# A fp32 diffusion step on one core: when the weight sums of seven-product blocks are made, where the last such block stands, and how the closing norm's factors are built

## The chip, the core and the metric

The kernel runs on one core of a Trainium2 chip. The metric is the device time of one execution in microseconds, the median of several runs. Five engines work side by side, each on its own queue in order: TensorE (PE, with its weight loads PEld), VectorE (DVE), ScalarE (ACT), GpSimd (POOL) and SyncE (SP), which here issues most DMAs.

## The reference

One layer of a hybrid diffusion backbone runs over 128 context tokens and 256 latent tokens with 2048 channels. A mixing sub-layer comes first (gated linear attention, a Fourier branch, gates). What matters here is the second sub-layer and its norm:

```python
h = rmsnorm(x, lw['norm_pre_ffn']) * (1.0 + sc2) + sh2
ff = (jax.nn.silu(h @ lw['w_ffn_gate']) * (h @ lw['w_ffn_up'])) @ lw['w_ffn_down']
x = x + ga2 * rmsnorm(ff, lw['norm_post_ffn'])
```

The hidden width is 5632. Everything is fp32.

## The kernel before, in words

**Split products.** Every fp32 operand is split into two parts, hi and lo, and a product is three matmuls: hi with hi, hi with lo, lo with hi. A weight tile of 128x1024 arrives by DMA (`raw`, two buffers, or `u`/`u3s`, below), ACT casts it to `whi` (L1324), DVE subtracts to get `wlo` (L1325), and PE uses both. `whi` and `wlo` have four buffers each: when PE takes weight k, the split of weight k+3 is queued (`grab2`, L1330).

**The stages of the feed-forward layer.** The 5632 hidden channels are 11 chunks of 4 tiles. In each chunk there are gate projections g0 to g3 and up projections u0 to u3 of 48 matmuls each (L275, moving 128x384), and the hidden tile is made by ACT (SiLU) and DVE (`hfE`, L1349), then split (`hid_hi` on ACT, `hid_lo` on DVE). The down projection of a chunk is done one chunk later, in two blocks: the order is written out in `ffn_order` (L172 on). The first block (`d`, half 0) stands behind u1 of the next chunk, the second (`d`, half 1) behind g3.

**A seven-product block.** For the 256 latent tokens a block multiplies two-by-two pieces by a scheme of seven products instead of eight; the context tokens are done plainly beside it. A block has eight weights: four loaded ones, here called U0 to U3 (`uraw`, three in the tile `u`, one in `u3s`), and four made from them in place, T0 to T3. `combine(n)` (L1310) makes one of four sums on DVE, n = 0 and 1 on L1313, 2 and 3 on L1314: they overwrite, in turn, the places of U2, U1, U0 and U3. A sum may run only when the weight in its place has been split. T0, T1, T2, T3 are the places of U2, U1, U0, U3 after their sums. The block is 66 matmuls of 128x512 (L1379), in PSUM tiles `pdn`, added to `psums` (and parts of `u3s`) in SBUF by DVE (L1401, `out`), or copied there by ACT in chunk 1. Before the change `split_next` makes sum n just ahead of the split that precedes Tn's.

**Other work on DVE.** In most chunks DVE also accumulates a modulation column (`adacc`, L573) at fixed places. Seven additions that close the scheme after its last block wait in a list, `pend` (L1426); each weight that is taken pops one.

**The end.** The last chunk's down projection is done in four plain stages (`e`, 36 matmuls each, tiles `pde`, three token tiles t = 0, 1, 2). Each tile is added to its place by DVE (`tail_step`, L1437), ACT squares it and sums along the row into `ssq` (L1438), and DVE adds that to `r3` (L1440). After the last stage each token's factor is made from `r3` (square root on ACT, L1483, reciprocal on DVE, L1486), put on a diagonal matrix `dg` (L1488), and PE multiplies `psums` by it (`py`, L1511): this scales and transposes at once. A "turn" is one such product of one 128x128 piece; in the trace it is two passes of PE, as it is plain fp32. Output k of 16 needs three turns, t = 0, 1, 2; eight `py` buffers exist. DVE (L1537) or, for five of the 16, ACT and POOL (L1529, L1530) apply the last gate and the residual `x1b`, which SP reloads (L1453) into the place of the normalised input, and SP or ACT stores the result.

**What sets the order.** PE, ACT, DVE and POOL run in the order in which the code is written. SP's order is set by a scheduler until the last stage.

Of the kernel before, what the change touches and what calls it, by code (L numbers as in the profile page):

```python
# [14 lines left out]
AF = mybir.ActivationFunctionType  # L15
# [6 lines left out]
D = 2048  # L22
# [12 lines left out]
FC = 4  # L35
# [61 lines left out]
def tile_step(ctx: ExitStack, tc: tile.TileContext, a, o):  # L97
# [941 lines left out]
    with ExitStack() as s:  # L1039
# [245 lines left out]
        pend = []  # L1285

        def load_more():
            n = 0
# [27 lines left out]
        def split_next():  # L1316
            if not entries:
                return
            e = entries.pop(0)
            if entries and entries[0][0] == "T":  # L1320
                combine(entries[0][1])
            raw = e[1] if e[0] == "R" else uraw[(2, 1, 0, 3)[e[1]]]
            hi, lo = (wp.tile([P, G], F32R, tag=t, name=t, bufs=4) for t in ("whi", "wlo"))
            ACT.copy(hi, raw)  # L1324
            DVE.tensor_sub(lo, raw, hi.bitcast(F32))  # L1325
# [12 lines left out]
        hid, sgs, hfs = {}, {}, {}  # L1338
# [93 lines left out]
        r3 = pf.tile([P, 3], F32, name="r3")  # L1432
        dg = pf.tile([P, 3, P], F32, name="dg")

        def tail_step(t, n, p, done):

            DVE.tensor_add(f_at(t, n), f_at(t, n), p)  # L1437
            ACT.activation(hfs[NFC][:, 0:512], f_at(t, n), AF.Square, accum_out=ssq[:, t, done : done + 1])  # L1438
            if done:
                DVE.tensor_add(r3[:, t : t + 1], ssq[:, t, 0:1] if done == 1 else r3[:, t : t + 1], ssq[:, t, done : done + 1])  # L1440

        rate[0] = 0.25
        ada = paced(ada_rest((5,)), rate)
# [1 line left out]
        for kind, c, j in ffn_order[HEAD:]:  # L1445
            if kind == "d":
                down(c, j)
            elif kind == "e":
                if not done:
                    hfs[NFC] = pe.tile([P, FC * T], F32, tag="hf", name="hfE", bufs=1)  # L1450
                    x1b = actp.tile([P, KT, T], F32, tag="A_hi", name="x1b")
                    for q in range(4):
                        SP.dma_start(x1b[:, 4 * q : 4 * q + 4, :], x1_d[:, 4 * q : 4 * q + 4, :])  # L1453
                pool, tag = ((pss, "side"), (psm, "mm"))[done % 2]
                pt = [pool.tile([P, 512], F32, tag=tag, name="pde") for _ in range(3)]
                for kh in range(2):
                    w = grab2()
                    for t in range(3):
                        wmm(pt[t], [h[:, 2 * kh : 2 * kh + 2, t * P : (t + 1) * P] for h in hid[c]], w, kh == 0, kh == 1)
                        if kh:  # L1460
                            if done == 2:
                                while pend:
                                    pend.pop(0)()
                            if done < 3:
                                tail_step(t, j, pt[t], done)
                done += 1
            else:
                if (kind, c, j) == ("u", NFC - 1, FC - 1):
                    for _ in ada:
                        pass  # L1470
                    ACT.activation(tmp1, eps_t, AF.Sqrt)
                proj2(c, j, dst_of[kind])
# [5 lines left out]
        def add_last(t):  # L1478
            DVE.tensor_add(f_at(t, n), f_at(t, n), pt[t])
            ACT.activation(hfs[NFC][:, 0:512], f_at(t, n), AF.Square, accum_out=ssq[:, t, 3:4])  # L1480

        def factors(lo, hi):
            ACT.activation(r3[:, lo:hi], r3[:, lo:hi], AF.Sqrt, bias=eps_t[:, 0:1], scale=1.0 / D)  # L1483

        def diagonals(lo, hi):
            DVE.reciprocal(r3[:, lo:hi], r3[:, lo:hi])  # L1486
            for t in range(lo, hi):
                DVE.tensor_scalar_mul(dg[:, t, :], ident, r3[:, t : t + 1])  # L1488

        def add_ss(t):  # L1490
            DVE.tensor_add(r3[:, t : t + 1], r3[:, t : t + 1], ssq[:, t, 3:4])

        add_last(0)
        add_last(1)
        add_ss(0)
        factors(0, 1)
        add_last(2)
        diagonals(0, 1)
        add_ss(1)
        add_ss(2)  # L1500
        factors(1, 3)
        diagonals(1, 3)

        py = {}
        places = [(pss, "side")] * 5 + [(psm, "mm")] * 3
# [116 lines left out]
```

## Time and profile before

| what | value |
|---|---|
| median of 3 runs | 2020.71 us (2020.23 to 2021.46) |
| the profiled execution | 2022.62 us |
| its span on the core | 2020.8 us |
| PE busy | 1994.4 us, 99% |
| DVE busy | 1476.3 us, 73% |
| ACT busy | 851.6 us, 42% |
| DMA | 380.18 MB, mean 188 GB/s |
| mean granted TensorE clock | 0.997 |

Times inside the trace run from the span's start. A row of the timeline gives start, duration, engine, line, operation and tiles, and in brackets the idle time of the engine before it and what ended it. A duration includes the fill and drain of the engine's pipeline, so two instructions that follow each other without a wait can overlap a little. Matmuls overlap much more: what counts for them is the time from start to start. A row of stretches gives start and end, length, the busy time of each engine (with its number of instructions), the granted clock, the DMA share and GB/s.

### The profile page before, as it was taken

The page shows a single profiled execution, that of the slowest core. Times are in us where ns is not written, and L with a number is a line of the kernel's source. Part 1 is how long each engine was busy: PE and PEld are TensorE (multiplying, and loading weights), DVE is VectorE, ACT ScalarE, POOL GpSimd, SP SyncE. Part 2 cuts the span into 40 slices and gives each one's busy share as a digit, 9 for nine tenths or more (in the row PEclk, how much of TensorE's full clock was granted, in tenths as well). Part 3 has the DMA queues.
Part 4 walks back from the last instruction along what each step waited for, and adds up shares of the span by engine and source line. Part 5 has one row for each costly group of instructions (what it writes and reads, how often), then busy time and mean ns, then how long its engine had stood idle before and what let it go on. Part 6 is the DMA issues. An engine that isn't in the chain of part 4 may idle for free.

```text
span 2020.8 us, 29311 instructions
## 1 busy us (share of the span) xinstructions
PE 1994.4 (99%) x11652; PEld 1870.1 (93%) x11652; DVE 1476.3 (73%) x1892; ACT 851.6 (42%) x1217; POOL 31.3 (2%) x43
## 2 busy tenths in 40 slices
PE   8999999999999999999999999999999999999998
PEld 5779999999999999999999898989899999989986
DVE  5668888888667778866576868676777777766675
ACT  4233554444346544446353433333343333333343
POOL 0000000000000000003000000000000000000000
PEclk9999999999999999999999999999999999999999
DMA  9978777677646686546344445443535454434333
GB/s 390 360 248 268 232 247 249 222 227 249 215 153 222 230 286 194 192 146 225 129 150 143 156 136 167 133 147 130 173 128 165 139 167 138 141 116 135 125 108 143
DMA packets 124521, 380.18 MB, mean 188 GB/s; under 512 B 13788, under 2 KB 32412, under 8 KB 120032
## 3 DMA queue, kind: packets, MB, share of 16 engines
q1 hardware_dynamic: 123664, 377.33, 55.6%
q8 instruction: 91, 1.49, 0.3%
q10 hardware_dynamic: 720, 0.98, 0.1%
q14 instruction: 46, 0.38, 0.1%
HBM read 361.48 MB, written 16.78 MB: 187 GB/s over the span
## 4 chain that ended last, share of the span: by engine, by line
PE 85%; DVE 9%; DMA 3%; ACT 2%; issue 1%; POOL 0%; ACTq 0%; DVEq 0%; POOLq 0%
PE pmm L275 64%; PE pdn L1379 8%; PE pv L416 3%; DVE wlo L1325 3%; DMA raw<-in_w_br_gla 2%; PE pgm L399 2%; DVE psums L1401 1%; DVE u L1313 1%; PE pf L275 1%; PE px L434 1%; PE pmm L1244 1%; DMA raw<-in_w_d 1%; PE py L1511 1%; DVE u3s L1314 1%; DVE u L1314 1%
## 5 line engine op out<-in xcount | busy, mean ns | idle before, releaser
L275 PE MATMUL pmm<-A_hi,whi 128*128 128x384 f32 x2480 | 832.1, 336 | 0.0
L275 PE MATMUL pmm<-A_hi,wlo 128*128 128x384 f32 x2480 | 830.9, 335 | 0.0
L275 PE MATMUL pmm<-A_lo,whi 128*128 128x384 f32 x2480 | 829.0, 334 | 0.0
L275 PEld LDWEIGHTS pmm<-A_hi,wlo 128*128 128x128 f32 x2480 | 465.4, 188 | 4.8 <-DVE wlo L1325 4.8
L275 PEld LDWEIGHTS pmm<-A_hi,whi 128*128 128x128 f32 x2480 | 465.6, 188 | 3.8 <-issue 1.4
L275 PEld LDWEIGHTS pmm<-A_lo,whi 128*128 128x128 f32 x2480 | 465.6, 188 | 1.0
L1325 DVE TENSOR_TENSOR wlo<-raw,whi 128x1024 fp32r<-128x1024 f32 x175 | 214.3, 1225 | 210.4 <-ACT whi L1324 210.2
L1324 ACT CAST whi<-raw 128x1024 fp32r<-128x1024 f32 x175 | 181.7, 1050 | 293.2 <-DMA raw<-in_w_g 138.4
L573 DVE SCALAR_TENSOR_TENSOR adacc<-adaw,spad,adacc 128x1024 f32<-128x1024 f32 x240 | 297.2, 1280 | 0.5 <-DMA adaw<-in_w_ada 0.2
L241 ACT CAST whi<-raw 128x1024 fp32r<-128x1024 f32 x181 | 189.8, 1051 | 196.1 <-DMA raw<-in_w_gate 77.1
L242 DVE TENSOR_TENSOR wlo<-raw,whi 128x1024 fp32r<-128x1024 f32 x179 | 218.1, 1222 | 68.9 <-ACT whi L241 68.6
L1325 DVE TENSOR_TENSOR wlo<-u,whi 128x1024 fp32r<-128x1024 f32 x120 | 146.5, 1222 | 40.0 <-ACT whi L1324 38.6
L1324 ACT CAST whi<-u 128x1024 fp32r<-128x1024 f32 x120 | 126.1, 1051 | 110.2 <-DVE u L1313 32.4
L1379 PE MATMUL pdn<-wlo,hid_hi 128*128 128x512 f32 x280 | 111.2, 397 | 6.5 <-DVE wlo L1325 6.5
L1379 PE MATMUL pdn<-whi,hid_lo 128*128 128x512 f32 x280 | 109.5, 391 | 0.0
L1379 PE MATMUL pdn<-whi,hid_hi 128*128 128x512 f32 x280 | 109.1, 390 | 0.0
L1401 DVE TENSOR_TENSOR psums<-psums,pdn 128x512 f32<-128x512 f32 x126 | 84.0, 685 | 0.0
L1379 PEld LDWEIGHTS pdn<-wlo,hid_hi 128*128 128x128 f32 x280 | 52.5, 188 | 22.8 <-DVE wlo L1325 12.8
L301 ACT CAST hid_hi<-hfE 128x384 fp32r<-128x384 f32 x44 | 22.6, 513 | 112.8 <-DVE hfE L1349 112.8
L1379 PE MATMUL pdn<-wlo,S_hi 128*128 128x512 f32 x160 | 63.3, 396 | 1.4 <-DVE wlo L1325 1.4
L1379 PEld LDWEIGHTS pdn<-whi,hid_hi 128*128 128x128 f32 x280 | 52.6, 188 | 11.0 <-ACT sg L1342 0.4
L1379 PE MATMUL pdn<-whi,S_lo 128*128 128x512 f32 x160 | 62.3, 390 | 0.0
(330 smaller groups left out, 2189.4 us busy)
## 6 DMA issues: line engine op xcount, KB each, us to landing
adaw<-in_w_ada SPq DMA_DIRECT2D x128, 512.0 KB, 4.0
raw<-in_w_g SPq DMA_DIRECT2D x88, 512.0 KB, 4.4
raw<-in_w_u SPq DMA_DIRECT2D x88, 512.0 KB, 4.2
slab<-in_w_ada SPq DMA_DIRECT2D x32, 1024.0 KB
raw<-in_w_gate SPq DMA_DIRECT2D x64, 512.0 KB, 4.5
u<-in_w_d SPq DMA_DIRECT2D x60, 512.0 KB, 4.5
raw<-in_w_in SPq DMA_DIRECT2D x44, 512.0 KB, 3.8
raw<-in_w_out SPq DMA_DIRECT2D x32, 512.0 KB, 4.4
```

Of the source, the lines that this page charges most:

```text
L241: ACT.copy(hi, raw)
L242: sub = lambda: eng.tensor_sub(lo, raw, hi.bitcast(F32))
L275: PE.matmul(dst, w[wi][:, k * n + n0 : k * n + n0 + P], x[xi][:, k0 + k, :], start=first and k == 0 and j == 0, stop=last and k == kts - 1 ...
L301: ACT.copy(hi, src)
L399: PE.matmul(pgv[q : q + 32, :], spad[:, k, :], slab[k // (KT // 2)][:, k % (KT // 2), :], start=k < 4, stop=k >= KT - 4,)
L416: PE.matmul(pv[2 * t + g], hT[x_][:, kb, t * P : (t + 1) * P], w_[:, g * 512 : (g + 1) * 512], start=kb == 0 and j == 0, stop=kb == KT - 1 ...
L573: DVE.scalar_tensor_tensor(acc[:, c, :], w, spad[:, k, c : c + 1], acc[:, c, :], op0=ALU.mult, op1=ALU.add,)
L1314: lambda: DVE.tensor_add(w11, w11, w22), lambda: DVE.tensor_sub(w21, w21, w11))[n]()
L1324: ACT.copy(hi, raw)
L1325: DVE.tensor_sub(lo, raw, hi.bitcast(F32))
L1379: PE.matmul(dst, stat[x_][:, m, :], w[w_].rearrange("p (i k c) -> p i k c", i=2, k=2)[:, :, m, :], start=first and m == 0 and n == 0, stop ...
L1401: DVE.tensor_add(unit(j, x), unit(j, x), pt[x])
```

## The change

Four edits:

1. **Sums.** The sums 0, 1 and 2 are made right behind the split of U2, the sum 3 right behind the split of U3, instead of one ahead of each split.
2. **Last chunk's order.** The second block of chunk 9 stands behind u3 of chunk 10 instead of between g3 and u3. From that u3 on each taken weight pops two of the pending additions instead of one.
3. **Sums of squares.** They are added once per stage for all three token tiles, instead of one tile at a time.
4. **Factors.** After the last stage, root, reciprocal and diagonal go tile by tile: add 0, factor 0, add 1, diagonal 0, add 2, then factor and diagonal of 1 and of 2. PE does eight turns of tile 0, eight of tile 1, then one per output. Six of the 16 outputs go by ACT and POOL instead of five.

```diff
-            if c and j == FC - 1:
+            if c and j == FC - 1 and c < NFC - 1:
                 ffn_order.append(("d", c - 1, 1))
             ffn_order.append(("u", c, j))
+            if c == NFC - 1 and j == FC - 1:
+                ffn_order.append(("d", c - 1, 1))
...
-            if entries and entries[0][0] == "T":
-                combine(entries[0][1])
             raw = e[1] if e[0] == "R" else uraw[(2, 1, 0, 3)[e[1]]]
             hi, lo = (wp.tile([P, G], F32R, tag=t, name=t, bufs=4) for t in ("whi", "wlo"))
             ACT.copy(hi, raw)
             DVE.tensor_sub(lo, raw, hi.bitcast(F32))
             ready.append((hi, lo))
+            if raw is uraw[2] and e[0] == "R":
+                for n in range(3):
+                    combine(n)
+            elif raw is uraw[3] and e[0] == "R":
+                combine(3)
...
-            if pend:
-                pend.pop(0)()
+            for _ in range(1 if late_sums[0] else 2):
+                if pend:
+                    pend.pop(0)()
...
-            if done:
-                DVE.tensor_add(r3[:, t : t + 1], ssq[:, t, 0:1] if done == 1 else r3[:, t : t + 1], ssq[:, t, done : done + 1])
...
+                if done == 1:
+                    DVE.tensor_add(r3, ssq[:, :, 0], ssq[:, :, 1])
+                if done == 2:
+                    DVE.tensor_add(r3, r3, ssq[:, :, 2])
...
+        add_last(0, n, pt[0], 3)
+        factor(0)
+        add_last(1, n, pt[1], 3)
+        diagonal(0)
+        add_last(2, n, pt[2], 3)
+        for t in (1, 2):
+            factor(t)
+            diagonal(t)
...
-        for k in range(8):
-            turn(k, 0)
-        on_act = (1, 4, 7, 10, 12)
+        for t in range(2):
+            for k in range(8):
+                turn(k, t)
+        on_act = (1, 3, 6, 8, 11, 13)
         tmp, stores = {}, []
         for k in range(KT):
-            if k >= 8:
-                turn(k, 0)
-            turn(k, 1)
-            turn(k, 2)
+            for t in range(3) if k >= 8 else (2,):
+                turn(k, t)
```

`factor(t)` adds the last `ssq` to `r3` and takes the root; `diagonal(t)` makes the reciprocal and `dg`. `add_last` adds a tile and squares it.

How the order moves, first on DVE around a first block, before. The rows `wlo<-u` are the splits of U0 to U2 (x3) and later of T0, T1, T2; `wlo<-u3s` those of U3 and T3; `u<-u` and `u3s<-u3s,u` are the sums; what an instruction waits for stands in brackets.

```order
L1325 TENSOR_TENSOR wlo<-u_9272,whi 128x1024 [waits PE_49,Activation_49] x3
L1349 TENSOR_TENSOR hfE<-sg,pmm 128x384 [waits PE_49]
L302 TENSOR_TENSOR hid_lo<-hfE,hid_hi 128x384 [waits Activation_49]
L1313 TENSOR_TENSOR u_9272<-u_9272 128x1024
L1325 TENSOR_TENSOR wlo<-u3s,whi 128x1024 [waits Activation_49]
L1401 TENSOR_TENSOR psums<-psums,pdn 128x512 [waits PE_49]
L1313 TENSOR_TENSOR u_9272<-u_9272 128x1024 [waits DVE_49]
L1325 TENSOR_TENSOR wlo<-u_9272,whi 128x1024 [waits Activation_49]
L1314 TENSOR_TENSOR u_9272<-u_9272 128x1024 [waits DVE_49]
L1325 TENSOR_TENSOR wlo<-u_9272,whi 128x1024 [waits Activation_49]
```

The same place on DVE after the change:

```order
L1325 TENSOR_TENSOR wlo<-u_9272,whi 128x1024 [waits PE_49,Activation_49] x2
L1315 TENSOR_TENSOR u_9272<-u_9272 128x1024 [waits DVE_49] x2
L1316 TENSOR_TENSOR u_9272<-u_9272 128x1024 [waits DVE_49]
L1356 TENSOR_TENSOR hfE<-sg,pmm 128x384 [waits PE_49]
L304 TENSOR_TENSOR hid_lo<-hfE,hid_hi 128x384 [waits Activation_49]
L1325 TENSOR_TENSOR wlo<-u3s,whi 128x1024 [waits DMAHW3_49,Activation_49]
L1316 TENSOR_TENSOR u3s<-u3s,u_9272 128x1024 [waits DVE_49]
L1408 TENSOR_TENSOR psums<-psums,pdn 128x512 [waits PE_49]
L1325 TENSOR_TENSOR wlo<-u_9272,whi 128x1024 [waits Activation_49] x2
```

The first three sums have moved ahead of `hfE`, the fourth right behind U3's split, and all four now wait for DVE itself: for the instruction just ahead of each.

On DVE at the end of the last stage, before. `u3s` and `psums` with `pde` are the additions of tiles 0, 1, 2; `r_9290` is `r3`.

```order
L1437 TENSOR_TENSOR psums_9278<-psums_9278,pde 128x512
L1440 TENSOR_TENSOR r_9290<-r_9290,ssq 128x1
L1479 TENSOR_TENSOR u3s<-u3s,pde 128x512
L1479 TENSOR_TENSOR psums_9278<-psums_9278,pde 128x512
L1491 TENSOR_TENSOR r_9290<-r_9290,ssq 128x1
L1479 TENSOR_TENSOR u3s<-u3s,pde 128x512
L1486 RECIPROCAL r_9290<-r_9290 128x1
L1488 TENSOR_SCALAR dg<-ident,r_9290 128x128
L1491 TENSOR_TENSOR r_9290<-r_9290,ssq 128x1 x2
L1486 RECIPROCAL r_9290<-r_9290 128x2
L1488 TENSOR_SCALAR dg<-ident,r_9290 128x128 x2
```

The same place after:

```order
L1444 TENSOR_TENSOR psums<-psums,pde 128x512 x2
L1444 TENSOR_TENSOR psums_9278<-psums_9278,pde 128x512
L1474 TENSOR_TENSOR r_9290<-r_9290,ssq 128x3
L1444 TENSOR_TENSOR u3s<-u3s,pde 128x512
L1489 TENSOR_TENSOR r_9290<-r_9290,ssq 128x1
L1444 TENSOR_TENSOR psums_9278<-psums_9278,pde 128x512
L1493 RECIPROCAL r_9290<-r_9290 128x1
L1494 TENSOR_SCALAR dg<-ident,r_9290 128x128
L1444 TENSOR_TENSOR u3s<-u3s,pde 128x512
L1489 TENSOR_TENSOR r_9290<-r_9290,ssq 128x1
L1493 RECIPROCAL r_9290<-r_9290 128x1
L1494 TENSOR_SCALAR dg<-ident,r_9290 128x128
```

Where each addition had its own addition to `r3` behind it, three additions now follow each other, and tile 0's diagonal no longer stands behind the addition of tile 2.

On SP from the loads of the last block on, before (`x_d` is the saved residual, `raw<-in_w_d` the weights of the closing stages):

```order
L1299 DMA u_9272<-in_w_d 128x2x512 x3
L1299 DMA u3s<-in_w_d 128x2x512
L1305 DMA raw<-in_w_u 128x1024 x2
L1305 DMA raw<-in_w_g 128x1024 x2
L1305 DMA raw<-in_w_u 128x1024 x2
L1305 DMA raw<-in_w_d 128x2x512 x4
L1453 DMA x1b<-x_d 128x1536 x4
L1305 DMA raw<-in_w_d 128x2x512 x4
```

And after:

```order
L1301 DMA u_9272<-in_w_d 128x2x512 x3
L1301 DMA u3s<-in_w_d 128x2x512
L1307 DMA raw<-in_w_u 128x1024 x2
L1307 DMA raw<-in_w_g 128x1024 x2
L1307 DMA raw<-in_w_u 128x1024 x2
L1307 DMA raw<-in_w_d 128x2x512 x2
L1458 DMA x1b<-x_d 128x1536 x4
L1307 DMA raw<-in_w_d 128x2x512 x6
```

Two of the closing weight loads have moved behind the loads of the residual.

More of the change, by code (lines that the diff above doesn't have):

```diff
@@ L1284, in tile_step @@
         items = [("R", src) for _, src in srcs] + [x if isinstance(x, tuple) else ("R", x) for x in ffn_items]
-        pend = []
+        pend, late_sums = [], [True]
         def load_more():
@@ L1433, in tile_step, with add_last @@
         dg = pf.tile([P, 3, P], F32, name="dg")
-        def tail_step(t, n, p, done):
+        def add_last(t, n, p, done):
             DVE.tensor_add(f_at(t, n), f_at(t, n), p)
             ACT.activation(hfs[NFC][:, 0:512], f_at(t, n), AF.Square, accum_out=ssq[:, t, done : done + 1])
-            if done:
-                DVE.tensor_add(r3[:, t : t + 1], ssq[:, t, 0:1] if done == 1 else r3[:, t : t + 1], ssq[:, t, done : done + 1])
         rate[0] = 0.25
@@ L1464, in tile_step @@
                             if done < 3:
-                                tail_step(t, j, pt[t], done)
+                                add_last(t, j, pt[t], done)
+                if done == 1:
+                    DVE.tensor_add(r3, ssq[:, :, 0], ssq[:, :, 1])
+                if done == 2:
+                    DVE.tensor_add(r3, r3, ssq[:, :, 2])
                 done += 1
@@ L1471, in tile_step @@
                     ACT.activation(tmp1, eps_t, AF.Sqrt)
+                    late_sums[0] = False
                 proj2(c, j, dst_of[kind])
@@ L1476, in tile_step, with factor, diagonal @@
         n = ffn_order[-1][2]
[L1478 to L1502, printed above, removed]
+        def factor(t):
+            DVE.tensor_add(r3[:, t : t + 1], r3[:, t : t + 1], ssq[:, t, 3:4])
+            ACT.activation(r3[:, t : t + 1], r3[:, t : t + 1], AF.Sqrt, bias=eps_t[:, 0:1], scale=1.0 / D)
+        def diagonal(t):
+            DVE.reciprocal(r3[:, t : t + 1], r3[:, t : t + 1])
+            DVE.tensor_scalar_mul(dg[:, t, :], ident, r3[:, t : t + 1])
+        add_last(0, n, pt[0], 3)
[6 more added lines that the diff above has]
+            diagonal(t)
         py = {}
```

## Prediction

> **What bounds the kernel now.** I read the page first, then the list of waits from 1000 us on, then the timeline of PE and DVE around single blocks. "First block" is the seven-product block behind up projection 1 of a chunk, "second block" the one behind gate projection 3. U0 to U3 are the loaded weights in their order of use, T0 to T3 the products whose weights are sums; S is a block's first matmul.
>
> ```profile
> PE 1994.4 (99%) x11652; PEld 1870.1 (93%) x11652; DVE 1476.3 (73%) x1892; ACT 851.6 (42%) x1217; POOL 31.3 (2%) x43
> PEld pdn L1379 <- DVE wlo L1325: 18.0, 26, 1.1
> DVE hfE L1349 <- PE pmm L275: 19.9, 11, 2.0
> ```
>
> PE is the bound, so only two things count: where PE waits, and what follows its last long matmul. PE's weight loads wait 18.0 us for a `wlo` in these blocks, and DVE in the same stretch idles eleven times, 2.0 us at most, before `hfE`.
>
> ```profile
> 1009.03 0.39 PE L1379 MATMUL pdn<-whi,hid_hi 128*128 128x512 f32 x1
> 1024.03 0.33 PE L275 MATMUL pmm<-A_hi,whi 128*128 128x384 f32 x1
> 1599.88 0.39 PE L1379 MATMUL pdn<-whi,hid_hi 128*128 128x512 f32 x1
> 1615.03 0.50 PE L1379 MATMUL pdn<-wlo,hid_hi 128*128 128x512 f32 x1 [0.68 <-DVE wlo L1325]
> 1616.30 0.34 PE L275 MATMUL pmm<-A_hi,whi 128*128 128x384 f32 x1
> ```
>
> A block has 66 matmuls. The first one of all (PSUM copied out by ACT) takes 15.00 us, 0.2273 a matmul, without a wait; the first block of a later chunk takes 16.42. T3's second matmul, the 62nd, is the first that needs T3's `wlo`: due at S + 61 x 0.2273 = S + 13.87 = 1613.75, it comes at 1615.03, 1.28 late. The first blocks of chunks 2 to 10, nine of them, have this.
>
> ```profile
> 1596.88 1.23 DVE L1325 TENSOR_TENSOR wlo<-u,whi 128x1024 fp32r<-128x1024 f32 x1 [1.45 <-ACT whi L1324]
> 1600.08 0.56 DVE L1349 TENSOR_TENSOR hfE<-sg,pmm 128x384 f32<-128x384 f32 x1 [1.97 <-PE pmm L275]
> 1601.21 0.56 DVE L302 TENSOR_TENSOR hid_lo<-hfE,hid_hi 128x384 fp32r<-128x384 f32 x1 [0.58 <-ACT hid_hi L301]
> 1601.68 1.22 DVE L1313 TENSOR_TENSOR u<-u 128x1024 f32<-128x1024 f32 x1
> 1601.09 1.04 ACT L1324 CAST whi<-u3s 128x1024 fp32r<-128x1024 f32 x1
> 1613.76 1.22 DVE L1325 TENSOR_TENSOR wlo<-u3s,whi 128x1024 fp32r<-128x1024 f32 x1
> ```
>
> DVE rests 1.97 us after U2's split, 0.58 before `hid_lo`, and then works without a pause until T3's `wlo` ends at 1614.98. So the block does not wait because DVE has too much to do in the whole chunk (73% busy), but because its sums begin only when the block itself does.
>
> **First blocks: sums earlier.** No work is added or taken away; three sums move into the 1.97 us. But each sum now stands right behind the instruction whose tile it overwrites or reads, and waits for it: U2's split, sum 0, sum 1, and for the last sum U3's split. What such a self-wait costs:
>
> ```profile
> 1572.91 0.42 DVE L1355 TENSOR_TENSOR hfE<-hfE 128x256 f32<-128x256 f32 x1
> 1573.37 0.43 DVE L1356 TENSOR_TENSOR hfE<-hfE 128x256 f32<-128x256 f32 x1
> 1609.09 1.28 DVE L1401 TENSOR_TENSOR psums<-psums,pdn 128x512 f32<-128x512 f32 x2
> ```
>
> A dependent one starts 0.04 after the end (0.46 apart for 0.42); the two independent 0.68 us additions take 1.28, so they overlap by 0.08. A self-wait costs 0.12 us, four of them 0.48. The Trainium skill ("VectorE: DVE Perf Modes", "The DRAIN you can't avoid") says the opposite: a semaphore after every copy cost nothing extra. By it the sum below would be the first rival's; the rows above differ from it.
>
> A second cost is a new wait. Three sums take 3 x 1.26 = 3.8 us from 1598.15 on, so `hfE` starts at 1601.8, 1.7 late. Behind it on ACT stand `hid_hi` and the copy of U3, which now ends at 1603.92 (it began 1.01 behind `hfE`); DVE has finished `hid_lo` by 1603.5 and, with no sum left for this place, waits 0.5 for that copy. Nobody else waits for the late `hfE`: its hidden tile is used a chunk later. T3's `wlo` thus ends at 1614.98 - 1.97 + 0.48 + 0.5 = 1613.99, and PE goes on at 1614.04, 0.3 late instead of 1.28. Gain 1.0 a block, 9 x 1.0 = **9.0 us**. A self-wait behind a 1024-wide sum is not in the trace; between 0 and 0.2 each, nearest to the 256-wide row, I take 0.12; the ends give 1.28 and 0.7 a block.
>
> **Second blocks.** Here the same move meets a DVE without idle time:
>
> ```profile
> 1638.48 1.23 DVE L1325 TENSOR_TENSOR wlo<-u,whi 128x1024 fp32r<-128x1024 f32 x1 [1.31 <-ACT whi L1324]
> 1639.63 2.48 DVE L573 SCALAR_TENSOR_TENSOR adacc<-adaw,spad,adacc 128x1024 f32<-128x1024 f32 x2
> 1654.09 1.22 DVE L1325 TENSOR_TENSOR wlo<-u3s,whi 128x1024 fp32r<-128x1024 f32 x1
> 1641.49 0.39 PE L1379 MATMUL pdn<-whi,hid_hi 128*128 128x512 f32 x1
> 1145.30:1147.40 2.10, 1.98 (x2) 1.00 0.00 0
> 1738.10:1740.20 2.10, 1.86 (x2) 1.00 0.03 8
> ```
>
> T3's `wlo` ends at 1655.31 and PE wants it at 1641.49 + 13.87 = 1655.36: no slack. From U2's split to there DVE does not pause. That the sums go ahead of the two `adacc` changes nothing in that total; the four self-waits add 0.48, and PE waits for all of it. The late `adacc` (3.8 us) also holds back SP's next weight load for the modulation, and behind it the next block's U loads, which wait for T0's split anyway. The two last rows (busy time of L573 ahead of a second block) are the first and last of six blocks with `adacc` there and PSUM added by DVE: **loss** 6 x 0.48 = **2.9 us**. The other three hold 2 us of idle or ACT's copies and lose nothing. Bounds: 0 to 4.8 (self-waits of 0 and 0.2).
>
> **Last chunk's order.** PE:
>
> ```profile
> 1938.84 0.39 PE L1379 MATMUL pdn<-whi,hid_hi 128*128 128x512 f32 x1
> 1954.59 0.34 PE L275 MATMUL pmm<-A_hi,whi 128*128 128x384 f32 x1
> 1963.14 0.39 PE L1379 MATMUL pde<-whi,hid_hi 128*128 128x512 f32 x1
> 1998.25 0.39 PE L1379 MATMUL pde<-whi,hid_lo 128*128 128x512 f32 x1
> ```
>
> The last block takes 15.75 where 15.00 would do, the 144 closing matmuls 35.50 (to 1998.64) where 143 x 0.2273 + 0.39 = 32.89 would. The block moves behind up projection 3. Its sums then start some 2 us before it, as in a first block, so T3's split is ready at S + 13.9, just in time. The closing products find `hid` split a whole block earlier. In the closing stage DVE no longer waits for ACT inside each tile, so the splits of its weights are not held up, and there is room for the 7 leftover additions, now two per weight. On SP the four x1b loads now stand ahead of six closing weight loads instead of four; they start when PE is done with the normalised input and run under the 15 us block, so they cost nothing; without that cover they would delay a weight, as they may do now. The square-root table's load moves to where ACT idles. I take back 0.75 + 2.6, less 0.4: the first closing weight's split follows T3's and one addition, at S + 13.9 + 0.6 + 1.1 = S + 15.6, and is due at S + 15.2. **2.95 us** (0.5 to 3.4).
>
> **Squares and factors.** The tail:
>
> ```profile
> 1998.09 0.16 DVE L1440 TENSOR_TENSOR r<-r,ssq 128x1 f32<-128x1 f32 x1 [0.85 <-ACT hfE L1438]
> 1999.78 0.68 DVE L1479 TENSOR_TENSOR u3s<-u3s,pde 128x512 f32<-128x512 f32 x1
> 2000.55 0.63 ACT L1480 ACTIVATE hfE<-u3s 128x512 f32<-128x512 f32 x1 [0.88 <-DVE u3s L1479]
> 2001.30 0.16 DVE L1491 TENSOR_TENSOR r<-r,ssq 128x1 f32<-128x1 f32 x1 [0.25 <-ACT hfE L1480]
> 2002.24 0.16 DVE L1486 RECIPROCAL r<-r 128x1 f32<-128x1 f32 x1 [0.18 <-ACT r L1483]
> 2002.44 0.29 DVE L1488 TENSOR_SCALAR dg<-ident,r 128x128 f32<-128x128 f32 x1
> 2002.78 11.21 PE L1511 MATMUL py<-dg,psums 128*128 128x128 f32 x72 [4.14 <-DVE dg L1488]
> 2007.46 0.74 DVE L1537 SCALAR_TENSOR_TENSOR x1b<-py,mods,x1b 128x128 f32<-128x128 f32 x2 [3.34 <-PE py L1511]
> ```
>
> DVE waits 0.85 for ACT per tile, so a tile takes it 0.68 + 0.85 + 0.08 = 1.61 against PE's 6 x 0.2273 = 1.36, and it falls behind over two stages: tile 0's last addition starts at 1999.78, though its products ended 2.73 before 1998.64. With one sum of squares per stage, behind all three additions, it starts on time, 2.65 before PE's end E. Behind it: square +0.77, sum +0.75, root +0.2 (then tile 1's addition, 0.6), reciprocal at +2.2, diagonal +0.2, PE +0.34: E + 0.1 instead of E + 4.14. Tile 1's diagonal is there 2.3 later (its root stands behind tile 2's square), tile 2's 0.9 after that.
>
> ```profile
> 18.92:22.34 3.42, 1.67 (x10) 1.37 (x10) 2.77 (x7) 1.46 (x3) 0.00 (x0) 1.00 1.00 417
> 2002.07:2008.89 6.82, 6.11 (x28) 6.11 (x29) 2.07 (x9) 1.62 (x6) 0.00 (x0) 0.50 0.00 0
> 2009.00:2019.50 10.50, 7.67 (x69) 7.47 (x67) 6.97 (x20) 3.04 (x9) 5.00 (x5) 0.98 0.83 300
> ```
>
> After its 4.14 us rest PE runs at clock 0.50, 6.11/28 = 0.218 a pass; later 7.67/69 = 0.111. A turn is two passes. With the rest gone: tile 0's 8 turns until E + 1.9, tile 1's from its diagonal, E + 2.35, until 4.15, one turn of tile 2 and its drain 0.5, so the first output is read at E + 4.65 instead of 2007.46 = E + 8.82: 4.2 us. PE's idle time there, 0.1 and 0.45, is far from that of the first window row. From there to the end 13.38 us pass, and the stores use 0.83 of 10.50; a fed queue needs 8.7, which returns 1.6 of the 1.8. **5.8 us** (3.5 to 6.5); the sixth output on ACT costs nothing under the stores.
>
> **Sum:** 9.0 - 2.9 + 2.95 + 5.8 = 14.9. The profiled execution took 2022.62 (span 2020.8), 1.9 over the median of 2020.71; it would take 2007.7, and the median **2005.8 us**.
>
> **Rivals.** (1) Self-waits free: first blocks 1.28 each, 11.5, no losses: 11.5 + 3.35 + 5.8 = 20.7, 2000.0; with waits at a block's first weights gone too, 1998. For: the page cited; against: the 0.46 spacing. 22%. (2) The timed runs keep their clock: the first output is 20 passes x 0.107 = 2.1 earlier there already, so the gain is 12.8: 2007.9. The 1.9 us between profile and median speaks for it; against it, the first window row: a window with PE busy 1.67 of 3.42 was followed by 0.50, so a 4.14 us rest does it wherever it falls. The Trainium skill ("TensorE: Matmul & The Clock Gate", "Part 1") wants a whole idle window of about 3.4 us, which the rest need not cover; the row differs. 12%. (3) The new tail starts at clock 0.50 all the same: 2 x 8 x 0.21 = 3.4 back, 2009.2. 5%. (4) What first blocks gain is lost at the weights behind them, whose loads hang on the same splits: 9.0 back, 2014.8; but those splits come earlier by as much as PE. 7%. (5) Slower: the self-wait x is longer behind 1024-wide sums. Its place is the run from U2's split to T3's. A first block gains 1.46 - 4x, a second one loses 4x, the first closing weight 4x: the whole is 22.2 - 64x with the terms above. From x = 0.35 on it is a loss; at 0.42 it is 4.7, and the time 2025.4. The rows above speak against it: 0.12. 4%. (6) The change does not do what it says, as PE's waits hang on something that the trace puts down to DVE wrongly: 2020.7. Against it: T3's split ends 0.05 before PE goes on. 3%.
>
> **Chances.** Forecast 47%. The range, 1998 to 2012, takes in (1), (2), (3) and the bounds of first and second blocks. 0.2% is 4 us, about what a measurement here can tell from no change: faster 0.93, same 0.03, slower 0.04.
>
> **What would show it.** Right: first blocks of 15.4 us, second ones of 15.6, four sums 1.26 apart behind U2, closing stage 33 us, PE's rest under 1 us, clock 1.00 in the tail. Wrong: second blocks still 15.14 (rival 1), or first blocks still over 16.

## The result, and the profile after

The changed kernel takes 2006.87 us (median of 4 runs, 2006.08 to 2009.9), the kernel before 2020.47 in the runs beside it: a ratio of 0.9936, 95% interval 0.9919 to 0.9953. That is 13.6 us less; 14.9 were forecast, and 2005.8 as the time. The profiled execution took 2006.71 us with a span of 2004.9, against 2022.62 and 2020.8 before. The page after, first lines, and then the first row of the list of waits of PE's weight loads from 1000 us on (us in total, times, longest):

```profile
span 2004.9 us, 29287 instructions
PE 1987.6 (99%) x11652; PEld 1868.2 (93%) x11652; DVE 1481.5 (74%) x1887; ACT 852.7 (43%) x1220; POOL 32.2 (2%) x44
```

```profile
PEld pdn L1386 <- DVE wlo L1325: 10.2, 17, 1.1
```

The work is the same; PE's weight loads wait 10.2 us for a `wlo` in the blocks instead of 18.0. What is left shows in single blocks.

The timeline of DVE and PE around the first block of chunk 7 (S = 1595.49) after the change; it answers to the rows at S = 1599.88 of before:

```profile
1593.76 2.48 DVE L1315 TENSOR_TENSOR u<-u 128x1024 f32<-128x1024 f32 x2
1596.28 1.23 DVE L1316 TENSOR_TENSOR u<-u 128x1024 f32<-128x1024 f32 x1
1599.50 1.23 DVE L1325 TENSOR_TENSOR wlo<-u3s,whi 128x1024 fp32r<-128x1024 f32 x1 [0.40 <-ACT whi L1324]
1608.30 1.22 DVE L1325 TENSOR_TENSOR wlo<-u3s,whi 128x1024 fp32r<-128x1024 f32 x1
1595.49 0.39 PE L1386 MATMUL pdn<-whi,hid_hi 128*128 128x512 f32 x1
1609.57 0.50 PE L1386 MATMUL pdn<-wlo,hid_hi 128*128 128x512 f32 x1
1610.84 0.33 PE L277 MATMUL pmm<-A_hi,whi 128*128 128x384 f32 x1
```

The three sums fill the 1.97 us that DVE rested and push `hfE` back by 1.7 us; they are 1.26 apart (1593.76 to 1596.28 is two of them). T3's split ends at 1609.52 = S + 14.03, PE goes on at S + 14.08, and the block takes 1610.84 - 1595.49 = 15.35 instead of 16.42. Eight of the nine first blocks are like this.

The second block at S = 1636.05, which answers to S = 1641.49 of before:

```profile
1634.30 2.49 DVE L1315 TENSOR_TENSOR u<-u 128x1024 f32<-128x1024 f32 x2
1637.96 2.47 DVE L575 SCALAR_TENSOR_TENSOR adacc<-adaw,spad,adacc 128x1024 f32<-128x1024 f32 x2
1649.15 1.22 DVE L1325 TENSOR_TENSOR wlo<-u3s,whi 128x1024 fp32r<-128x1024 f32 x1
1636.05 0.39 PE L1386 MATMUL pdn<-whi,hid_hi 128*128 128x512 f32 x1
1650.42 0.50 PE L1386 MATMUL pdn<-wlo,hid_hi 128*128 128x512 f32 x1 [0.34 <-DVE wlo L1325]
1651.71 0.33 PE L277 MATMUL pmm<-A_hi,whi 128*128 128x384 f32 x1
```

Here T3's split ends at S + 14.32 instead of 13.82, PE waits, and the block takes 15.66 instead of 15.14.

The one left, in chunk 3, is another matter. On ACT and then DVE:

```profile
1192.92 1.05 ACT L1324 CAST whi<-raw 128x1024 fp32r<-128x1024 f32 x1 [1.59 <-DMA raw<-in_w_u]
1194.00 1.23 DVE L1325 TENSOR_TENSOR wlo<-raw,whi 128x1024 fp32r<-128x1024 f32 x1 [2.09 <-ACT whi L1324]
1196.28 2.47 DVE L575 SCALAR_TENSOR_TENSOR adacc<-adaw,spad,adacc 128x1024 f32<-128x1024 f32 x2
1201.06 2.48 DVE L1315 TENSOR_TENSOR u<-u 128x1024 f32<-128x1024 f32 x2
```

DVE waits for a copy on ACT, which itself waited 1.59 us for its load, and then has the two `adacc` between U0's split and U1's; the first sum starts 0.81 ahead of S = 1201.87 instead of 1.73, and the block takes 16.29. With the sums made late (the kernel before, and the run with the sums undone below) this block is as long as the others, 16.4: there DVE still has a rest that can take up such a delay.

The end, on DVE and then PE:

```profile
1987.28 0.29 DVE L1494 TENSOR_SCALAR dg<-ident,r 128x128 f32<-128x128 f32 x1
1992.17 1.00 DVE L1537 SCALAR_TENSOR_TENSOR x1b<-py,mods,x1b 128x128 f32<-128x128 f32 x3 [1.46 <-PE py L1512]
1987.17 0.39 PE L1386 MATMUL pde<-whi,hid_lo 128*128 128x512 f32 x1
1987.62 0.49 PE L1512 MATMUL py<-dg,psums 128*128 128x128 f32 x2
```

The closing products end at E = 1987.56; the first turn starts 0.06 later instead of 4.14, and the first output is read at 1992.17 = E + 4.61 instead of E + 8.82. And a stretch near the start, first of before, then of after (start and end, length, busy time of PE, PEld, DVE, ACT, POOL, granted clock, DMA share, GB/s):

```profile
22.34:25.75 3.41, 3.41 (x25) 1.88 (x27) 1.39 (x3) 0.00 (x0) 0.00 (x0) 0.50 1.04 411
```

```profile
22.34:25.75 3.41, 3.41 (x40) 2.07 (x39) 1.80 (x3) 0.20 (x1) 0.00 (x0) 1.00 1.02 406
```

In the tail the turns run 0.11 us apart a pass (two take 0.49 with the drain), so clock 0.50 is gone there. At the start, where nothing was changed, before's profile had a window of 0.50 and after's had none: the first block of all starts 2.12 us earlier (1006.91 against 1009.03) for that alone. That is chance between two executions, not the change: the changed kernel, profiled once more (last run below), had such a window too and began its first block at 1008.26. The difference of the spans, 15.9, is then:

| part | forecast | measured |
|---|---|---|
| nine first blocks | 9.0 | 8.7 (147.82 - 139.10) |
| six second blocks | -2.9 | -3.0 (90.94 - 93.96) |
| last block, the projections around it, closing products | 2.95 | 3.0 |
| tail behind E | 5.8 | 4.8 (22.16 - 17.34) |
| other blocks and projections | 0 | 0.3 |
| up to the first block | 0 | 2.1 |

Without the last line it is 13.8.

### The profile page after: what moved, and what is told of

Same layout as the page of the kernel before. It is cut to its first block, busy times and chain, and to the rows that moved or that the text cites. A ratio compares the mean times of both kernels' runs of the same rounds, so it can differ in the third digit from the quotient of the medians.

```text
span 2004.9 us, 29287 instructions
## 1 busy us (share of the span) xinstructions
PE 1987.6 (99%) x11652; PEld 1868.2 (93%) x11652; DVE 1481.5 (74%) x1887; ACT 852.7 (43%) x1220; POOL 32.2 (2%) x44
## 3 DMA queue, kind: packets, MB, share of 16 engines
q10 hardware_dynamic: 864, 1.18, 0.2%
## 4 chain that ended last, share of the span: by engine, by line
PE 85%; DVE 11%; issue 2%; ACT 2%; DMA 1%; POOL 0%; DVEq 0%; ACTq 0%; POOLq 0%
PE pmm L277 64%; PE pdn L1386 5%; DVE wlo L1325 5%; PE pv L418 3%; DVE psums L1408 2%; PE pf L277 2%; PE pde L1386 2%; PE pgm L401 1%; ACT whi L1324 1%; PE px L436 1%; DVE u3s L1316 1%; PE pmm L1246 1%; DVE u L1315 1%; DVE adacc L575 1%; DMA raw<-in_w_g 1%
## 5 line engine op out<-in xcount | busy, mean ns | idle before, releaser
L1386 PE MATMUL pdn<-whi,S_hi 128*128 128x512 f32 x160 | 62.4, 390 | 0.0
```

The costliest lines, as they stand in the source:

```text
L1386: PE.matmul(dst, stat[x_][:, m, :], w[w_].rearrange("p (i k c) -> p i k c", i=2, k=2)[:, :, m, :], start=first and m == 0 and n == 0, stop ...
```

## The experiments

Each ran beside the kernel before on the same chip. Line numbers in the rows are those of the kernel that ran.

**Each edit undone, alone.** The four kernels are the changed one with one edit taken back to the code of before.

*Sums.* Edit:

```diff
             e = entries.pop(0)
+            if entries and entries[0][0] == "T":
+                combine(entries[0][1])
...
-            if raw is uraw[2] and e[0] == "R":
-                for n in range(3):
-                    combine(n)
-            elif raw is uraw[3] and e[0] == "R":
-                combine(3)
```

> The changed kernel, with the sums made as before, one ahead of each split (the three other edits stay). Theory: this edit alone gained 8.7 us in nine first blocks and lost 3.0 in six second ones; undone, first blocks go back to 16.4 us, second ones to 15.14, and the last block, which now stands behind up projection 3 and is a block of the first kind, takes 16.4 instead of 15.34, with up to 1 us more at the closing weights behind it. 2006.9 + 8.7 - 3.0 + 1.1 (to 2.1) = 2013.7 to 2014.7. Rival (the gain at first blocks is given back at the weights behind them and came from elsewhere): 2006.9.

Measured: 2014.45 us (7 runs), 0.9973 of before, interval 0.9962 to 0.9984. Against 2006.87 that is 7.6. The first blocks take 16.41 again, second ones 15.14, the last one 16.41. The projections between the blocks take as long with early sums as with late ones: from the first block to the closing products all that is not a block takes 639.0 us with them, 639.2 here, 639.4 before. So nothing that a first block gains is given back behind it, and the rival that said so falls.

*Last chunk's order.* Edit: the block back behind gate projection 3, one pending addition per weight.

> The changed kernel, with the last second block back between gate projection 3 and up projection 3 and one pending addition per weight. Theory: the closing 144 products take 35.5 us again instead of 33.2, since their hidden tile is split only just ahead of them; the block itself, now with early sums and without modulation work, takes 15.0 to 15.2. 2006.9 + 2.3 - 0.2 = 2009.0 (2008.5 to 2009.9). Rival (the closing stage was slow because DVE waited for ACT at each tile's sum of squares, which stays mended here): 2007.

Measured: 2010.14 us (5 runs, 2007.67 to 2010.58), 0.9946, interval 0.9934 to 0.9959: 3.3 more than the changed kernel, just over the expected range; the two intervals overlap, so it is the profile that shows the cause. The last block takes 15.00, the closing products 35.55 instead of 33.18. PE's loads there:

```profile
PEld pde L1384 <- ACT hid_hi L301: 1.2, 1, 1.2
PEld pde L1384 <- DVE wlo L1323: 1.1, 1, 1.1
```

The late split of the hidden tile is there, as in the theory; and the sums of squares, which stay mended, do not help the closing products. PE also rests 1.48 us behind them: DVE still has pending additions when the last tiles are due, so this edit also feeds the tail, which is 0.9 longer. This kernel's first blocks in chunks 3 and 4 took 16.67 and 16.57; the edit does not touch them, and they differ between two profiles of one kernel as well (last run below).

*Sums of squares.* Edit:

```diff
+            if done in (1, 2):
+                DVE.tensor_add(r3[:, t : t + 1], ssq[:, t, 0:1] if done == 1 else r3[:, t : t + 1], ssq[:, t, done : done + 1])
...
-                if done == 1:
-                    DVE.tensor_add(r3, ssq[:, :, 0], ssq[:, :, 1])
-                if done == 2:
-                    DVE.tensor_add(r3, r3, ssq[:, :, 2])
```

> The changed kernel, with each tile's sum of squares added behind its own addition again. Theory: DVE waits 0.85 us for ACT at each tile and falls behind PE; tile 0's last addition starts about 2 to 2.7 us late, PE rests 2 us or more ahead of the diagonal products, and the first output is read by as much later: 2009 to 2009.6; 2011 if the rest also brings clock 0.50. Rival (with the last chunk's order mended DVE starts the closing stages without a backlog, so the waits stay hidden): under 2007.5.

Measured: 2011.95 us (5 runs, 2008.21 to 2012.15), 0.9953, interval 0.994 to 0.9965: 5.1 more by the medians. Its timeline of DVE and PE, and two stretches of PE:

```profile
1988.02 0.16 DVE L1447 TENSOR_TENSOR r<-r,ssq 128x1 f32<-128x1 f32 x1 [0.85 <-ACT hfE L1445]
1989.62 0.16 DVE L1447 TENSOR_TENSOR r<-r,ssq 128x1 f32<-128x1 f32 x1 [0.85 <-ACT hfE L1445]
1989.70 0.68 DVE L1444 TENSOR_TENSOR u3s<-u3s,pde 128x512 f32<-128x512 f32 x1
1992.43 0.58 PE L1510 MATMUL py<-dg,psums 128*128 128x128 f32 x1 [2.86 <-DVE dg L1492]
```

```profile
1988.87:1992.28 3.41, 0.70 (x4) 0.24 (x2) 1.77 (x6) 1.94 (x6) 0.00 (x0) 1.00 0.00 0
1992.28:1995.69 3.41, 3.26 (x15) 3.26 (x16) 1.73 (x8) 1.72 (x6) 0.00 (x0) 0.50 0.00 0
```

DVE waits 0.85 per tile and steps 1.60 where PE steps 1.36; tile 0's last addition starts at 1989.70, behind E = 1989.58. PE rests 2.86 us and then runs at half the clock; the first output is read at E + 8.50. That is the mechanism of the theory's upper case, but not its size. The tail behind E is 3.4 us longer than in the changed kernel, where 4.1 were forecast; another 1.7 of the profile's difference lie ahead of the first block (it starts at 1008.57, not 1006.91), where this edit changes nothing. The timed runs lie near 2008.5 and near 2012, so their median is no good measure of this edit.

*Factors and turns.* Edit: the old order of additions, roots and diagonals, eight turns of tile 0 and then tiles 1 and 2 per output, five outputs on ACT.

> The changed kernel, with roots, reciprocals and diagonals in the old order (tile 0's diagonal behind tile 2's addition, one root for tiles 1 and 2), the old order of turns and five outputs on ACT. Theory: with the sums of squares on time only the place of tile 0's diagonal counts; it comes 0.7 to 0.9 us later, tile 2's hardly, and the stores bound the rest: 2007.2 (2006.5 to 2008). Rival (tile by tile is what took the rest away): PE rests 2 us and more, clock 0.50 again, 2010 to 2011.7.

Measured: 2006.06 us (5 runs), 0.9929, interval 0.9917 to 0.9942. The theory had it 0.3 us slower than the changed kernel; it isn't, and by its profile it is faster (the timed runs alone can't tell 0.8 us). PE, then DVE:

```profile
1988.78 1.94 PE L1517 MATMUL py<-dg,psums 128*128 128x128 f32 x15 [1.18 <-DVE dg L1497]
1989.90 0.48 DVE L1497 TENSOR_SCALAR dg<-ident,r 128x128 f32<-128x128 f32 x2
1991.32 0.74 DVE L1541 SCALAR_TENSOR_TENSOR x1b<-py,mods,x1b 128x128 f32<-128x128 f32 x2 [0.94 <-PE py L1517]
```

PE rests 1.18 us and yet the first output is read at 1991.32 = E + 3.71, 0.9 sooner than with edit 4. The clock stays at 1.00: this rest of 1.18 did not bring the slow one. The tail behind E is 16.39 long instead of 17.34.

**Fewer turns first.** If that is because eight turns of tile 1 stand ahead of tile 2's first one, four of them should do as well:

```diff
-        for t in range(2):
-            for k in range(8):
+        for t, m in ((0, 8), (1, 4)):
+            for k in range(m):
                 turn(k, t)
...
                 turn(k, t)
+            if k < 4:
+                turn(k + 4, 1)
```

> The changed kernel, but PE does only four turns of tile 1, not eight, ahead of the first turn of tile 2; the other four follow one by one. Theory (from the run with edit 4 undone: its first output was read 0.8 us sooner though PE rested 1.1 us): the first output stands behind tile 1's eight turns; with four it is read at E + 3.8 instead of E + 4.6, and since the stores bound the rest, the whole is 0.8 shorter: 2006.1. Rival (the start of the stores doesn't set the end): 2006.9.

Measured: 2006.11 us (5 runs), 0.9932, interval 0.9919 to 0.9944. The first output is read at E + 3.74, and the tail is 16.36 long. The theory holds to 0.1 us in the profile; 0.8 us is too little for the timed runs to show by themselves.

**Self-waits.** Is it the wait behind the instruction just ahead that costs, or something else in the new order of the second blocks?

```diff
                                 acc[:, c, :], w, spad[:, k, c : c + 1], acc[:, c, :], op0=ALU.mult, op1=ALU.add,
                             )
+                        if due_sums:
+                            sum_fn[0](due_sums.pop(0))
...
             if raw is uraw[2] and e[0] == "R":
-                for n in range(3):
-                    combine(n)
-            elif raw is uraw[3] and e[0] == "R":
+                blk[0] += 1
+                if blk[0] % 2 or blk[0] == 2 * NFC - 2:
+                    for n in range(3):
+                        combine(n)
+                else:
+                    due_sums.extend(range(4))
+            elif raw is uraw[3] and e[0] == "R" and not due_sums:
                 combine(3)
+            elif due_sums:
+                combine(due_sums.pop(0))
```

> The changed kernel, but in the second blocks that have modulation work no sum stands right behind the instruction that it waits for: the order is split of U2, adacc, sum 0, adacc, sum 1, split of U3, sum 2, split of T0, sum 3. The work and the semaphore waits are the same. Theory (a self-wait costs 0.12 us only behind the instruction just ahead of it): T3's split ends at S + 13.82 again, as before the change, and the six blocks take 15.14 instead of 15.66: 3.1 us, 2003.8 where the changed kernel takes 2006.9. Rival (the wait itself costs, wherever it stands, or the late split of U3 and the late adacc do it): 15.6, and no change in time.

Measured: 2011.94 us (5 runs), 0.996, interval 0.9948 to 0.9973: 5 us slower, where 3.1 faster was expected. The blocks with `adacc` did what the theory says:

```profile
1636.63 1.22 DVE L1318 TENSOR_TENSOR u<-u 128x1024 f32<-128x1024 f32 x1
1637.77 1.28 DVE L576 SCALAR_TENSOR_TENSOR adacc<-adaw,spad,adacc 128x1024 f32<-128x1024 f32 x1
1649.90 1.22 DVE L1330 TENSOR_TENSOR wlo<-u3s,whi 128x1024 fp32r<-128x1024 f32 x1
1637.30 0.39 PE L1397 MATMUL pdn<-whi,hid_hi 128*128 128x512 f32 x1
1652.44 0.34 PE L278 MATMUL pmm<-A_hi,whi 128*128 128x384 f32 x1
```

From a sum's start to the next instruction's 1.14 pass, as 1.22 less the 0.08 of overlap, where it took 1.26 behind its like. T3's split ends at S + 13.82, and all six blocks take 15.13 to 15.16. The waits are all still there; with an instruction between they cost nothing. U3's split also comes earlier here than in the changed kernel (S + 2.80, not S + 4.31), so the length of the block by itself would not rule out that its place counts; but DVE works without a pause from U2's split to T3's in both, and what differs is the spacing of the four sums. The loss came from elsewhere: in the two second blocks that have no `adacc`, the edit put each sum behind the split ahead of its own weight's, so that ACT's copy stood waiting for it:

```profile
1837.94 1.05 ACT L1329 CAST whi<-u 128x1024 fp32r<-128x1024 f32 x1 [2.50 <-DVE u L1318]
1841.49 1.05 ACT L1329 CAST whi<-u 128x1024 fp32r<-128x1024 f32 x1 [2.50 <-DVE u L1318]
```

Sum, copy and split then run one after the other, 3.55 a weight, and these two blocks take 18.26 and 18.79 instead of 15.09 and 15.00: 7.0 us lost against the 3.1 gained, and at the end of the second one begins a window at clock 0.50.

**Third sum later.** What ends the first blocks at 15.35 is DVE's wait for ACT's copy of U3, which the late `hfE` brings:

```diff
-                for n in range(3):
-                    combine(n)
+                blk[0] += 1
+                if blk[0] % 2 or blk[0] == 2 * NFC - 2:
+                    combine(0)
+                    combine(1)
+                    due_up.append(2)
+                else:
+                    for n in range(3):
+                        combine(n)
...
             DVE.tensor_mul(hf[:, j, :], sgs.pop(j), p)
+            if due_up:
+                combine(due_up.pop())
```

> The changed kernel, but in first blocks and in the last block sum 2 stands behind hfE instead of ahead of it. Theory: hfE starts 1.1 us earlier, so the copy of U3 on ACT behind it is done when DVE wants it (0.4 us of waiting gone) and one self-wait goes too: T3's split ends at S + 13.5 instead of S + 14.03, ahead of PE's S + 13.87, and the blocks take 15.0. 9 x 0.34, and 0.5 more where a late load in chunks 3 and 4 had made the block longer: 3.1 to 4, 2003 to 2003.8 against 2006.9. Rival (what PE waits for is not T3's split): still 15.35, 2006.9.

Measured: 2001.3 us (4 runs), 0.9909, interval 0.9895 to 0.9922: 5.6 less than the changed kernel, more than expected.

```profile
1593.79 0.55 DVE L1363 TENSOR_TENSOR hfE<-sg,pmm 128x384 f32<-128x384 f32 x1
1594.25 1.22 DVE L1317 TENSOR_TENSOR u<-u 128x1024 f32<-128x1024 f32 x1
1595.87 1.22 DVE L1326 TENSOR_TENSOR wlo<-u3s,whi 128x1024 fp32r<-128x1024 f32 x1
1604.67 1.22 DVE L1326 TENSOR_TENSOR wlo<-u3s,whi 128x1024 fp32r<-128x1024 f32 x1
```

The block starts at 1593.12. Sum 2 now covers the 0.58 us that DVE waited for `hid_hi` as well, which the expectation had missed: T3's split ends at S + 12.77, 1.1 ahead of PE, and all nine first blocks take 15.00, those of chunks 3 and 4 too. The projections behind the blocks take 2.1 us less in all: PE's loads there wait 1.6 us for a `wlo` instead of 4.3.

**The rest and the clock.** In the kernel before, PE's rest is filled with matmuls that nobody reads, so that only the clock changes:

```diff
+        pool, tag = places[0]
+        py[0] = pool.tile([P, T], F32, tag=tag, name="py")
+        warm(py[0], 12)
         for k in range(8):
             turn(k, 0)
```

> The kernel before, with 12 matmuls of 128x384 whose results nobody reads put into PE's rest ahead of the first turn (3.9 us of the 4.14; nothing else is changed). Theory (the rest brings the slow clock): the clock stays at 1.00, a pass takes 0.11 instead of 0.21 us, the first output is read 2.0 us earlier, and the time falls by 2.0 against the kernel before, in the timed runs too: ratio 0.9990. Rival (the timed runs keep their clock through the rest): the profile as above, but the timed runs the same as before. Rival (the slow clock has nothing to do with the rest): 0.50 again, no change.

Measured: 2022.58 us (11 runs), 1.001, interval 1.0001 to 1.0019: no gain. The 12 matmuls took two passes each, 24 x 0.32 = 7.7 us where 4.14 were free; the first output was read at E + 10.01. The clock was 1.00. So once more with 6:

> The kernel before, with 6 instead of 12 unread matmuls in PE's rest (in the run with 12 each took two passes of 0.32 us, 7.7 us in all, so the first turn came 3.6 us late; the clock stayed at 1.00). Theory: 12 passes fill 3.9 of the 4.14 us, the turns start when they did before and run at clock 1.00; from the first turn to the first output's read 2.4 us instead of 4.68. The time falls by 2.3 to 2.9 us against the kernel before, in the timed runs too. Rival (the timed runs keep their clock through the rest): the profile as above, the timed runs the same as before.

Measured: 2018.69 us (11 runs), 0.9989, interval 0.998 to 0.9998, 2.3 less than the kernel before beside it. Its rows from the first turn on, and the stretch of turns:

```profile
2002.00 0.38 PE L1511 MATMUL py<-dg,psums 128*128 128x128 f32 x1 [0.27 <-DVE dg L1488]
2004.54 0.74 DVE L1540 SCALAR_TENSOR_TENSOR x1b<-py,mods,x1b 128x128 f32<-128x128 f32 x2 [1.21 <-PE py L1511]
```

```profile
2002.07:2004.50 2.43, 2.43 (x22) 2.43 (x23) 0.81 (x4) 0.32 (x2) 0.00 (x0) 1.00 0.00 0
```

The first turn starts at E + 4.14 as before; 2.54 later, not 4.68, the first output is read. So of the 4.2 us by which the change brings the first output forward, the slow clock was 2.1. The timed runs have it too, though with an interval that only just leaves out no change (its upper end is 0.4 us less): the rival that they keep their clock becomes unlikely.

**All of it in one kernel.** Sum 2 behind `hfE` in first blocks, the sums of second blocks spaced by the `adacc` (without `adacc` in the places of before), the old factors and turns:

> What the runs so far point to, in one kernel: the changed kernel with sum 2 behind hfE in first blocks, with the sums of the second blocks spaced by the adacc (and, where there is no adacc, each sum one split ahead of its own again, as before the change), and with the old order of factors and turns. Theory: 2006.9 - 5.6 (third sum later, as measured) - 3.1 (six second blocks at 15.14) - 0.8 (first output at E + 3.8) = 1997.4. If first and second blocks take from each other: 1999 to 2001.

Measured: 1997.15 us (4 runs, 1996.93 to 1997.32), 0.9879 of before, interval 0.9866 to 0.9893. First blocks take 15.00, second ones 15.13 to 15.16, the closing products 32.80. PE's own waits from the first block to the last turn, the whole list:

```profile
PE py L1533 <- DVE dg L1513: 1.2, 1, 1.2
```

> The changed kernel once more, beside the two above on the same chip: 2006.9, ratio 0.9936. If the first blocks of chunks 3 and 4 depend on when loads land, their lengths differ from the first profile (16.29 and 15.37), and the other seven are 15.35 again.

Measured: 2008.13 us (5 runs, 2006.61 to 2010.07), 0.9932, interval 0.9918 to 0.9945. The first blocks of chunks 3 and 4 took 16.49 and 16.28, the other seven 15.34 to 15.37. `joined` is thus 11.0 us faster than the changed kernel beside it, and 23.9 faster than the kernel before.

## Why the prediction was right

**First blocks.** Right in each step: T3's split S + 14.1 forecast (1613.99) and S + 14.03 measured, block 15.4 and 15.35, four self-waits of 0.12, the new wait for U3's copy 0.5 and 0.40. Not seen was the block of chunk 3: the 8.7 measured are eight blocks that gain 1.07 each, where 1.0 was forecast, and one that gains 0.13. By filling DVE's rest the change makes T3's split depend on when a load lands some 9 us ahead of the block; in chunks 3 and 4 the block took 15.34 to 16.67 in the profiles with all three sums early, different from run to run.

**Second blocks.** Right: 15.6 forecast, 15.66 measured, six of them. The spaced sums show the cause: with the same waits and an instruction between, 15.14. The first rival, self-waits free, falls: a semaphore wait is free here only when what it waits for is not the instruction just ahead. The Trainium skill ("VectorE: DVE Perf Modes", "The DRAIN you can't avoid") has a row of copies in which a semaphore after each cost nothing extra. The sums here differ from that, by 0.12 each. The slower rival needed 0.35 or more; 0.12 was measured behind 1024-wide sums too. Of the others, the loss behind the first blocks falls by the 639 us that all but the blocks takes with either order, the slow clock in the new tail by its clock of 1.00, and a wait wrongly put down to DVE by the blocks that did get shorter.

**Last chunk's order.** 2.95 forecast, 3.0 measured, but that the sums agree is partly luck. The block was to go from 15.75 to 15.00, with T3's split just in time; it takes 15.34, like a first block, and gains 0.4 instead of 0.75. The closing products gain 2.3 where 2.2 was forecast, and 0.25 comes from the projections around the block, which the forecast had at nothing. The main cause, the hidden tile split earlier, holds by the run without the edit. That the sums of squares help the closing products does not hold: with the squares undone they take 33.19, as with them. The run without the edit adds a cause: the pending additions done earlier also free DVE for the last tiles.

**Tail.** The mechanism was right, and so was the first output's place, E + 4.65 forecast and E + 4.61 measured. The step that failed is "a fed queue needs 8.7, which returns 1.6 of the 1.8": only 0.6 came back. The stores from their first packet on, in stretches, after:

```profile
1993.79:2002.50 8.71, 5.27 (x48) 5.08 (x46) 5.18 (x16) 2.95 (x9) 5.35 (x6) 1.00 1.00 356
2002.50:2003.50 1.00, 0.00 (x0) 0.00 (x0) 0.00 (x0) 0.00 (x0) 0.00 (x0) 1.00 0.17 51
2003.50:2004.94 1.44, 0.00 (x0) 0.00 (x0) 0.00 (x0) 0.00 (x0) 0.00 (x0) 0.50 0.00 0
```

And before:

```profile
2009.08:2018.50 9.42, 7.59 (x68) 7.39 (x67) 6.97 (x20) 2.96 (x9) 5.00 (x5) 1.00 0.86 309
2018.50:2019.52 1.02, 0.00 (x0) 0.00 (x0) 0.00 (x0) 0.00 (x0) 0.00 (x0) 0.81 0.64 235
```

In both, 1.62 us pass from the first read to the first packet. After the change the queues are then full for 8.71 us, which is just what was forecast. But the forecast left 0.2 us for running out, and the last packets take 1.00 us more at a share of 0.17, where before the last 1.02 us had a share of 0.64; the time behind them is 0.1 longer, 1.44 instead of 1.32. That is 0.9 of the 1.0 us that did not come back, and most of the 1.1 by which the sum missed the 13.8. Why the last packets come so late is not shown. From first read to end the other kernels with the changed end take 12.3 to 12.8 us, the two built on the kernel before 13.3 to 13.4, even with the clock at 1.00. Two of them with the same turns (edit 4 undone; six unread matmuls) have full queues until 11.0 us behind the first read, and then run out for 0.4 us in the one and 1.0 in the other; the cause stays open.

**What was lumped together.** The tail's terms had one sum for edits 3 and 4. The runs part them: by the profiles' tails, edit 3 is worth 3.4 us (5.1 by the medians of the timed runs), and edit 4 costs 0.9 to 1.0. Its eight turns of tile 1 stand ahead of tile 2's first turn, and with the sums of squares on time there was hardly a rest left for them to fill.

## What to carry to other kernels

Work moved into an engine's rest is worth what ends sooner on the engine that bounds the time; the same move, made where there is no rest, costs its own new waits. Put an instruction that has to run anyway between two that depend on each other. And undo a change edit by edit once it is measured: here one of the four worked against the other three, and undoing it was part of the fastest kernel.

## What the runs showed of the hardware

- The granted clock holds for multiples of 3.41 us in these traces (3.41, 6.83 and 13.65, for example), on a grid of each execution's own; a stretch that lies on the grid shows 1.00 or 0.50 and nothing between. By such stretches, a window in which PE was busy for 0.70 us (squares undone, above), 1.67 (the kernel before, near its start) or 1.79 (spaced sums, here) was followed by one at 0.50; one with 1.86 (fewer turns first, here) or 2.32 (the changed kernel, here) was not. An idle stretch of 1.75 us at the start is thus sometimes inside one window and sometimes split over two: nine of the 13 profiles have a window at 0.50 there and reach the first block at 1007.9 to 1009.0, four have none and reach it at 1006.2 to 1007.1. The Trainium skill ("TensorE: Matmul & The Clock Gate", "Part 1") asks for a whole idle window of about 3.4 us. These rows differ from it.

```profile
1848.38:1851.79 3.41, 1.79 (x7) 0.90 (x7) 3.41 (x6) 2.94 (x3) 0.00 (x0) 1.00 0.57 177
```

```profile
19.72:23.13 3.41, 1.86 (x9) 1.60 (x9) 2.79 (x7) 0.90 (x2) 0.00 (x0) 1.00 1.00 413
```

```profile
20.35:23.76 3.41, 2.32 (x13) 1.75 (x17) 2.76 (x6) 0.51 (x1) 0.00 (x0) 1.00 0.99 407
```

- On DVE an instruction of 1.22 us is followed by an independent one after 1.14, by one that waits for it after 1.26: 0.12 us for each wait on the instruction just ahead. The dependent one starts 0.04 behind the end at 1024 elements a row as at 256.
